# Scores by seven half products, silu read from the banks, and one bank per output tile in a hybrid decoder step

## The chip, the cores and the metric

The kernel runs on one core of one Trainium2 chip. The metric is the device time of one execution in microseconds (us); a time of several runs is their median.

## The reference, cut to what matters

One layer for 2048 new tokens (and 32 sample tokens of running requests), all in float32:

```python
def mixer(xn, s0, lp):
    q, k, v, r, a, u, sv = split_cols(xn @ w_in)
    logg = jax.nn.log_sigmoid(a @ w_alpha + b_alpha) / GLA_TAU
    o, S = gla_chunked(q, k, v, logg, s0)
    o = rmsnorm(o, g_gla_out).reshape(B, T, GLA_WIDTH) * jax.nn.silu(r)
    sv = rmsnorm(jax.nn.gelu(sv).reshape(B, T, SGU_HEADS, SGU_DH), g_sgu)
    s_out = jax.nn.gelu(u) * sgu_spatial(sv, w_s, b_s)
    return jnp.concatenate([o, s_out], axis=-1) @ w_out, S, sv

def mem_attend(hn, mk, mv, wq_x, wo_x):
    s = einsum('bthd,bmhd->bhtm', hn @ wq_x, mk) * MEM_DH ** -0.5
    return einsum('bhtm,bmhd->bthd', softmax(s), mv) @ wo_x

def layer(x, ...):
    h = x + mixer(rmsnorm(x, g_mix), ...)
    h = h + mem_attend(rmsnorm(h, g_x), ...)
    return h + conv_ffn(rmsnorm(h, g_ffn), ...)   # gate, up, causal conv, down
```

The model width is 1024 (eight tiles of 128), the width of the FFN 2816 (22 tiles), and the cross-attention has 4 heads over 256 memory tokens. A last RMS norm gives the output.

## The kernel before, in words

The 2048 tokens go in four blocks, s = 0 to 3, of 512; block 1 carries the 32 sample tokens through the mixer as well (544 columns, in two pieces of 272), block 2 through the FFN. Activations lie with features on partitions and tokens on columns, `B.h[m]` being the residual of feature tile m. Every large product runs on TensorE in three passes, `mm3` (L91 to L94): both operands are split into a high and a low part, and high by high, low by high and high by low are summed in one PSUM bank. `split` (L83) makes the high part on ACT and the low part on DVE. There are two pools of four banks, `acc` for the large sums and `mps` for all else.

A block goes through these stages: the input projections (tiles named t_ws, a_wk, a_wq, t_wv, a_wu, t_wr, and the narrow product `ap` of `a_fn`, L838), into which the steps of GLA (gated linear attention) and of SGU (the spatial gating) are woven; the output projection (a_wo); `stat` (the row sums for the norm); the scores (sc); the turns (transposes of the softmaxed scores, pT); the attention's output (a_wx); the FFN (a_wg, a_wup, then down, d). `weave` (L458) spreads side lists of steps over a main list by their index, and `run` requests the weights of steps ahead of time; behind both, the framework's scheduler lays out each engine's instructions, and each engine then works in that order.

Four places matter below.

*Scores.* In block 0 the memory keys are multiplied into the query weights (`fold_qk`, L595), so that a score is one product of the normed residual with a table `qkd` of 1024 x 512 for each pair of heads. `score(i, j)` adds up, for pair i, eight k-tiles by four token chunks of 128, each mm3 with 512 columns moving: 192 products a block. `soften` reads the banks: row maximum (DVE), exponential (ACT), reciprocal and scaling (DVE).

*Seven products.* The gate and up products of the FFN already go by seven products in place of eight half-size ones, after Strassen: `seven_tokens` (L181) makes, from an even and an odd k-tile of activations, the four sums and their splits that go to the tiles named w, wb, wt and wu.

*r and its silu.* The projection t_wr gives r, token-major, in four `mps` banks. DVE scales them into SBUF (L828, "r<-t_wr"), and later `silu(c)` (L1142) in the tail of GLA applies silu in place on ACT. The tail is: squares of o (ACT, "junk<-o"), `ors` (POOL), the gates (DVE, L1148, o by ors by r), transposes `otp`, and the splits ch and cl that the output projection reads for k-tiles 0 to 3.

*Output projection.* `out_proj_steps` first adds k-tiles 4 to 7 (those of SGU) for all eight output tiles, each half into `h` (L1208): 96 products. Then, in w2, k-tiles 0 to 3, another 96. With `whole=True`, as the attention's output has it, a tile's bank stays open over both halves, and only output tiles 0 to 3 can start early (48 products), since four banks are open.

At the end of the last block, `down_last` does the last two FFN tiles in two token halves, so that `final_steps` (transposes yp, squares, norm, y) of one half can follow while the other is computed.

## Time and profile before

| | |
|---|---|
| median of 3 runs | 2845.88 us (2843.69 to 2846.43) |
| the profiled execution | 2846.04 us |
| its span, first to last instruction | 2844.3 us |
| granted TensorE clock, mean share | 0.997 |
| busy: PE, weight loads (PEld), DVE, ACT, POOL | 99%, 86%, 62%, 37%, 19% |
| main DMA queue, share of 16 engines | 64.6% |

The span lies 1.7 us inside the execution's own time. "Busy" is the time in which at least one instruction of an engine ran; matmuls overlap in their pipeline, so the pace of a run of products is read from the distance between their starts, not from the length of one. A bracket behind a row is the idle time of that engine before it, and the instruction that ended it.

### The profile page before, as it was taken

What the parts mean: (1) busy time and instruction counts of PE and PEld (TensorE: products, weight loads), DVE (VectorE), ACT (ScalarE), POOL (GpSimd) and SP (SyncE); (2) the same over time, 40 slices, a digit from 0 to 9 for tenths busy, and PEclk for the clock granted to TensorE, in tenths of its full rate; (3) what the DMA queues carried; (4) which work ended last, traced back from release to release, by engine and by line L of the source; (5) the groups of instructions that cost most, each with busy time, mean ns of one, the idle gap of its engine ahead of it and who ended that gap; (6) DMA issues with size and microseconds to landing.
All of it is one profiled execution on the core that took longest, in us unless ns stands there. A gap on an engine that the chain in (4) does not pass through costs nothing.

```text
span 2844.3 us, 45766 instructions
## 1 busy us (share of the span) xinstructions
PE 2814.4 (99%) x17366; PEld 2457.6 (86%) x17366; DVE 1773.6 (62%) x3160; ACT 1047.0 (37%) x1942; POOL 542.4 (19%) x617
## 2 busy tenths in 40 slices
...
GB/s 304 207 156 199 208 228 332 335 340 329 345 112 77 94 153 178 302 284 291 329 344 161 73 60 181 191 259 257 257 263 213 104 69 119 185 258 269 273 286 173
DMA packets 363920, 625.54 MB, mean 220 GB/s; under 512 B 26730, under 2 KB 235724, under 8 KB 363702
## 3 DMA queue, kind: packets, MB, share of 16 engines
q1 hardware_dynamic: 363702, 622.62, 64.6%
q8 instruction: 138, 2.26, 0.3%
q14 instruction: 80, 0.66, 0.1%
...
## 4 chain that ended last, share of the span: by engine, by line
PE 95%; DVE 2%; DMA 1%; ACT 1%; issue 1%; POOL 0%; SPq 0%; DVEq 0%; POOLq 0%; ACTq 0%
PE d L92 6%; PE d L94 6%; PE d L93 6%; PE a_wo L92 2%; PE a_wo L94 2%; PE a_wo L93 2%; PE sc L94 2%; PE sc L93 2%; PE sc L92 2%; PE a_wx L93 2%; PE a_wx L94 2%; PE a_wx L92 2%; PE s L1022 2%; PE a_wg L92 1%; PE a_wup L92 1%; PE a_wg L93 1%
## 5 line engine op out<-in xcount | busy, mean ns | idle before, releaser
L92 PE MATMUL d<-acth,whi_wd 128*128 128x512 f32 (+2 forms) x720 | 244.6, 340 | 0.5 <-DVE h L1581 0.5
L93 PE MATMUL d<-actl,whi_wd 128*128 128x512 f32 (+2 forms) x720 | 242.5, 337 | 0.0
L94 PE MATMUL d<-acth,wlo_wd 128*128 128x512 f32 (+2 forms) x720 | 242.0, 337 | 0.0
L1581 DVE TENSOR_TENSOR h<-d,h 128x512 f32<-128x512 f32 (+1 forms) x232 | 133.4, 582 | 139.6 <-PE d L94 139.4
L1520 POOL TENSOR_TENSOR c<-c,bc_f 128x512 f32<-128x512 f32 (+1 forms) x88 | 138.5, 1578 | 137.9 <-ACT c L1519 137.2
L94 PEld LDWEIGHTS d<-acth,wlo_wd 128*128 128x128 f32 x720 | 135.4, 188 | 15.3 <-issue 1.2
L92 PEld LDWEIGHTS d<-acth,whi_wd 128*128 128x128 f32 x720 | 135.3, 188 | 14.4 <-DVE h L1581 0.7
L93 PEld LDWEIGHTS d<-actl,whi_wd 128*128 128x128 f32 x720 | 135.6, 188 | 13.8 <-issue 0.4
L1510 ACT ACTIVATE c<-g,colsb 128x512 f32<-128x512 f32 x88 | 71.7, 815 | 203.7 <-DVE g L1479 151.8
L1542 POOL TENSOR_TENSOR c<-r_q_wup,c 128x512 f32<-128x512 f32 (+1 forms) x33 | 59.1, 1790 | 333.5 <-DVE r_q_wup L279 213.1
L92 PE MATMUL a_wo<-ch,h_wo 128*128 128x512 f32 (+1 forms) x320 | 112.7, 356 | 4.5 <-DVE r L828 4.5
L1507 POOL COPY carry<-g 128x2 f32<-128x2 f32 x88 | 30.7, 349 | 436.5 <-DVE g L1479 434.4
L94 PE MATMUL a_wo<-ch,l_wo 128*128 128x512 f32 (+1 forms) x320 | 112.4, 353 | 0.0
L93 PE MATMUL a_wo<-cl,h_wo 128*128 128x512 f32 (+1 forms) x320 | 112.0, 351 | 0.0
L1511 DVE SCALAR_TENSOR_TENSOR c<-g,colsb,c 128x512 f32<-128x512 f32 x88 | 86.0, 977 | 29.3 <-ACT c L1510 28.8
L92 PE MATMUL sc<-whi_qk,woh 128*128 128x512 f32 x256 | 102.1, 399 | 0.0
L92 PE MATMUL a_wx<-pTh,whi_wx 128*128 128x512 f32 x256 | 101.3, 396 | 0.0
L94 PE MATMUL sc<-whi_qk,wol 128*128 128x512 f32 x256 | 101.1, 397 | 0.0
L93 PE MATMUL a_wx<-pTl,whi_wx 128*128 128x512 f32 x256 | 101.1, 395 | 0.0
L93 PE MATMUL sc<-wlo_qk,woh 128*128 128x512 f32 x256 | 101.0, 395 | 0.0
L94 PE MATMUL a_wx<-pTh,wlo_wx 128*128 128x512 f32 x256 | 100.6, 393 | 0.0
L84 ACT ACTIVATE acth<-c 128x512 fp32r<-128x512 f32 (+1 forms) x88 | 55.9, 636 | 110.4 <-DVE c L1542 85.0
...
## 6 DMA issues: line engine op xcount, KB each, us to landing
...
```

Of the source, the lines that this page charges most:

```text
L84: act.activation(hi, src, AF.Copy)
L92: pe.matmul(ps, wh, xh, start=first, stop=False)
L93: pe.matmul(ps, wh, xl, start=False, stop=False)
L94: pe.matmul(ps, wl, xh, start=False, stop=last)
L1022: pe.matmul(ps3[:, :, c * 64:(c + 1) * 64], kl[:, c * 128:(c + 1) * 128], kr3[:, :, c * 64:(c + 1) * 64], start=True, stop=True)
L1507: pool.tensor_copy(carry[:, f, :], g[:, SB:SB + 2])
L1510: act.activation(c[:, :SB], g[:, 2:SB + 2], AF.Identity, bias=cb, scale=w2)
L1511: dve.scalar_tensor_tensor(c[:, :SB], g[:, 1:SB + 1], w1, c[:, :SB], ALU.mult, ALU.add)
L1520: pool.tensor_tensor(c[:, :T], c[:, :T], B.fbc[:, :T], ALU.mult)
L1542: (dve, pool)[i].tensor_tensor(c[:, :T], q[i], c[:, :T], ALU.mult)
L1581: dve.tensor_tensor(B.h[m + mm][:, cs], ps[:, :cw], B.h[m + mm][:, cs], ALU.add)
```

## The change

Four parts that belong together in the code. The scores use seven products of halves (halves of the tokens, even and odd k-tiles, the two heads of a pair); the table becomes `q7d`, with the plain parts stored split and the sums S1 to S4 stored whole and split when they are loaded; the seven results are put together by additions on DVE into `B.p`, and `soften` reads those. The output projection of blocks 0, 2 and 3 uses `whole`. Silu of r is applied by ACT as it reads the t_wr banks, and the `silu` steps in the tail are gone. The key-value products of GLA for four chunks go into one bank (`states`), the chunks' outputs two to a bank (`chunks`). Besides, `a_fn` stands after the t_ws steps and uses an `mps` bank, and the end of the last block is written differently: the last two FFN tiles token-major (`last_rows`), h transposed ahead (`turn_h`). The core of the diff:

```diff
-    def seven_tokens(a, b, H, name):
+    def seven_tokens(a, b, H, name, apart=False):
...
         lo_, hi_ = slice(0, H), slice(H, 2 * H)
+        one = U(f"w1{name}", F32R)
+        split(one[:, lo_], one[:, hi_], B11)
+        out = {"A11": (one[:, lo_], one[:, hi_])}
         dve.tensor_tensor(t13[:, lo_], B12, B11, ALU.subtract)
+        th, tl = U(f"wth{name}", F32R), U(f"wtl{name}", F32R)
+        if apart:
+            split(th[:, lo_], tl[:, lo_], t13[:, lo_])
         dve.tensor_tensor(t13[:, hi_], B22, B12, ALU.subtract)
         dve.tensor_tensor(t24[:, lo_], B22, t13[:, lo_], ALU.subtract)
         dve.tensor_tensor(t24[:, hi_], B21, t24[:, lo_], ALU.subtract)
-        one = U(f"w1{name}", F32R)
-        split(one[:, lo_], one[:, hi_], B11)
...
-            split(h[:, :2 * H], l[:, :2 * H], src[:, :2 * H])
+        for nm, src, first, second in (("b", b, "A12", "S4"), ("u", t24, "S2", "A22"), ("t", t13, "S1", "S3")):
+            if nm == "t":
+                h, l, c = th, tl, slice(H if apart else 0, 2 * H)
+            else:
+                h, l, c = U(f"w{nm}h{name}", F32R), U(f"w{nm}l{name}", F32R), slice(0, 2 * H)
+            split(h[:, c], l[:, c], src[:, c])
             out[first], out[second] = (h[:, lo_], l[:, lo_]), (h[:, hi_], l[:, hi_])
...
+            t13, t24 = U(f"q13{h}{j}{kk}"), U(f"q24{h}{j}{kk}")
+            dve.tensor_tensor(t13[:, m0], f[:, m0], f[:, m1], ALU.add)
+            dve.tensor_tensor(t13[:, m1], e[:, m0], f[:, m0], ALU.subtract)
+            dve.tensor_tensor(t24[:, m0], t13[:, m0], e[:, m0], ALU.subtract)
+            dve.tensor_tensor(t24[:, m1], e[:, m1], t24[:, m0], ALU.subtract)
+            for i, t in enumerate((t13, t24)):
+                put(sums[:, 2 * i:2 * i + 2, jj], t[:, :512].rearrange("p (s m) -> p s m", s=2))
...
         def a_fn():
             B.aT = T_(f"aT{s}")
             for ci, (c0, cw) in enumerate(chunks_of(sample)):
-                ps = acc(f"ap{s}{ci}")
+                ps = mps(f"ap{s}{ci}")
...
-        out.insert(3, Step(a_fn))
+        out.append(Step(a_fn))
...
-        out += tm_steps(w, R0, xs, sample, ev_tm("r", scaled), f"wr{s}")
+        out += tm_steps(w, R0, xs, sample, ev_tm("r", lambda o, i, f: act.activation(o, i, AF.Silu, scale=f)), f"wr{s}")
...
+        def states(p):
+            kv = mps(f"kv{s}{p}")
+            for c in range(4):
+                for hh in range(2):
+                    h = 2 * p + hh
+                    pe.matmul(kv[hh * 64:(hh + 1) * 64, c * 128:(c + 1) * 128],
+                              B.kt[p][:, c * 128 + hh * 64:c * 128 + (hh + 1) * 64],
+                              B.v[c][:, h * 128:(h + 1) * 128], start=True, stop=True)
+            t = U(f"S{s}{p}")
+            B.S[p] = [state[p]] + [t[:, c * 128:(c + 1) * 128] for c in range(3)]
+            state[p] = cp.tile([128, 128], F32, tag=f"S{p}", name=f"S{s}{p}e", bufs=2)
+            for c in range(4):
+                dve.scalar_tensor_tensor(B.S[p][c + 1] if c < 3 else state[p], B.S[p][c], B.eb[p][:, c:c + 1],
+                                         kv[:, c * 128:(c + 1) * 128], ALU.mult, ALU.add)
...
+        def chunks(p, i):
...
-        def silu(c):
-            n = 128 if c < 4 else NS
-            act.activation(B.r[c][:n, :512], B.r[c][:n, :512], AF.Silu)
...
-            out += [lambda p=p, c=c: chunk(p, c) for c in range(4)]
+            out += [lambda p=p: states(p)] + [lambda p=p, i=i: chunks(p, i) for i in range(2)]
...
-        tail = [onorm] + [lambda c=c: silu(c) for c in range(nt)] + [lambda c=c: gate(c) for c in range(nt)]
+        tail = [onorm] + [lambda c=c: gate(c) for c in range(nt)]
...
-        def score(i, j):
+        SEQ = ("A11", "S1", "A12", "S2", "S3", "S4", "A22")
+        def score(i, nm):
+            plain, sums = q7d[i]
             def fn(wu):
                 wh, wl = wu
...
+                if nm == "A11":
+                    B.p[i], B.ps = [None] * 4, {}
+                ps = B.ps[nm] = acc(f"sc{s}{i}{nm}")
+                for c in range(2):
                     cs = slice(c * 128, (c + 1) * 128)
...
-            return Step(fn, [wready(qkd[i][j], f"qk{s}{i}{j}")])
...
-        def soften(i, c, ps):
...
+                    for k in range(4):
+                        xh, xl = B.hn[k][nm]
+                        mm3(ps[:, c * 256:(c + 1) * 256], xh[:, cs], xl[:, cs], wh[:, k], wl[:, k], k == 0, k == 3)
+                q = B.p[i]
+                plus = lambda o, nm, b: dve.tensor_tensor(q[o][:, :512], B.ps[nm], q[b][:, :512], ALU.add)
+                if nm == "A11":
+                    q[0] = T_(f"p{s}{i}0")
+                    act.activation(q[0][:, :512], ps, AF.Copy)
+                elif nm == "S2":
+                    q[3], q[1] = T_(f"p{s}{i}3"), T_(f"p{s}{i}1")
+                    plus(3, "S2", 0)
+                    plus(0, "A12", 0)
+                    plus(1, "S1", 3)
+                    soften(i, 0)
+                elif nm == "S3":
+                    q[2] = T_(f"p{s}{i}2")
+                    plus(2, "S3", 3)
+                    plus(3, "S3", 1)
+                    soften(i, 3)
+                elif nm == "S4":
+                    plus(1, "S4", 1)
+                    soften(i, 1)
+                elif nm == "A22":
+                    plus(2, "A22", 2)
+                    soften(i, 2)
+            def load():
+                if nm in PLAIN:
+                    return wready(plain[:, PLAIN.index(nm)], f"qk{s}{i}{nm}")()
+                raw = wraw(f"qk{s}{i}{nm}")
+                nc.sync.dma_start(raw[:, :1024], sums[:, SUMS.index(nm)].rearrange("p k m -> p (k m)"))
+                return wsplit(raw[:, :1024].rearrange("p (k m) -> p k m", k=4), f"qk{s}{i}{nm}")
+            return Step(fn, [load])
+        def soften(i, j):
+            mx = narrow(f"mx{s}{i}{j}")
+            p, c0 = B.p[i][j], 2 * (j % 2)
+            dve.tensor_reduce(mx[:, 0:2], p[:, :512].rearrange("p (t m) -> p t m", t=2), AX.X, ALU.max)
+            dve.tensor_tensor(mx[:, 0:2], mx[:, 0:2], B.rn[:, c0:c0 + 2], ALU.mult)
+            for c in range(2):
+                pt = p[:, c * 256:(c + 1) * 256]
+                act.activation(pt, pt, AF.Exp, bias=mx[:, c:c + 1], scale=B.rp[:, c0 + c:c0 + c + 1],
...
+        def turn_h(j):
+            for c in range(4):
+                ps = mps(f"hp{c}{j}")
+                for i in range(4):
+                    pe.transpose(ps[:, i * 128:(i + 1) * 128], B.h[4 * j + i][:, c * 128:(c + 1) * 128], ident)
+                t = U(f"ht{c}{j}")
+                act.activation(t[:, :512], ps, AF.Copy)
+                cur["ht", c, j] = t
+        def last_rows(*ws):
...
+            for c in range(4):
+                cs = slice(c * 128, (c + 1) * 128)
+                ss = narrow(f"yss{s}{c}")
+                for j in range(2):
+                    wh, wl = ws[j]
+                    ps = acc(f"dr{s}{c}{j}")
                     for k in range(2):
...
+                        hi, lo = acts[FT - 2 + k]
+                        mm3(ps, hi[:, cs], lo[:, cs], wh[:, k], wl[:, k], k == 0, k == 1)
+                    y = cur["ht", c, j]
...
+                dve.tensor_tensor(ss[:, 2:3], ss[:, 0:1], ss[:, 1:2], ALU.add)
+                rstd_of(ss[:, 3:4], ss[:, 2:3], 128, 1, 1.0 / D)
+                if ready:
+                    finish(*ready)
+                ready = c, ss
+            finish(*ready)
...
-            if fin and nf == 2:
-                pend = [down_last(f0, lambda half: fin[2 * half:2 * half + 2])]
+            if last and nf == 2:
+                pend = [Step(lambda j=j: turn_h(j)) for j in range(2)]
+                pend.append(Step(last_rows, [wready(wdd[f0, 4 * j], f"wd{s}{f0}{j}") for j in range(2)]))
             else:
...
-                                      lambda B=B: B.cat, "gx", "wo", B.mix_sample, 4, B.mix_sample, keep)
+                                      lambda B=B: B.cat, "gx", "wo", B.mix_sample, 4, B.mix_sample, keep, seven=True, whole=not B.mix_sample)
         folds = [(qk_steps, 0, 10), (vo_steps, 11, 19)] if s == 0 else []
...
-        steps += weave(sc + x1, (turns[:2], 4, 5), (turns[2:], 8, 8))
-        fin = final_steps(B)
...
         else:
-            steps += fmain[-4:] + conv_out_steps(carry, 2, o_state_conv[0, 0], "nc") + flast
+            steps += fmain[-4:-2] + flast[:1] + fmain[-2:] + ncs[4:] + flast[1:]
```

On ACT, in block 2, this is where the tail of GLA begins; `h_wo` is the high part of a weight tile of the output projection, `junk` a square of o, `ch26` and `ch27` are high parts of SGU's outputs. Before:

```order
L84 ACTIVATE ch26_16507<-z22_16504 128x512
L84 ACTIVATE ch27_16549<-z23_16546 128x512
L1142 ACT_TABLE_LOAD
L1142 ACTIVATE r20_16565<-r20_16565 128x512
L1142 ACTIVATE r21_16566<-r21_16566 128x512
L1142 ACTIVATE r22_16567<-r22_16567 128x512
L1142 ACTIVATE r23_16568<-r23_16568 128x512
L84 ACTIVATE h_wo201_16618<-r_wo201_16616 128x1024
L84 ACTIVATE h_wo202_16668<-r_wo202_16666 128x1024
```

And now:

```order
L84 ACTIVATE h_wo242_17148<-r_wo242_17146 128x1024
L879 ACTIVATE junk_90,oss2_17184<-o22_16650 128x128 x2
L84 ACTIVATE ch27_17142<-z23_17139 128x512
L879 ACTIVATE junk_90,oss2_17184<-o22_16650 128x128
L874 ACT_TABLE_LOAD
L874 ACTIVATE r20_17158<-t_wr20_16985,xrs2_15606 128x512
L874 ACTIVATE r21_17159<-t_wr21_16992,xrs2_15606 128x512
L874 ACTIVATE r22_17160<-t_wr22_16999,xrs2_15606 128x512
L874 ACTIVATE r23_17161<-t_wr23_17006,xrs2_15606 128x512
L879 ACTIVATE junk_90,oss2_17184<-o23_16651 128x128 x4
L84 ACTIVATE h_wo202_17215<-r_wo202_17213 128x1024
```

The four activations of r now read the banks `t_wr`, behind one more `h_wo` and the table load, and in front of four squares of o; before they worked in SBUF, and DVE had emptied the banks.

On TensorE, in block 2, the change of the score products, from the last products of the output projection on. Before:

```order
L94 MATMUL a_wo2070_16966<-ch23_16732,l_wo203_16739 128x512
L92 MATMUL sc200_17004<-whi_qk200_16770,woh20_16820 128x512
L93 MATMUL sc200_17004<-wlo_qk200_16772,woh20_16820 128x512
L94 MATMUL sc200_17004<-whi_qk200_16770,wol20_16821 128x512
L92 MATMUL sc200_17004<-whi_qk200_16770,woh21_16842 128x512
L93 MATMUL sc200_17004<-wlo_qk200_16772,woh21_16842 128x512
L94 MATMUL sc200_17004<-whi_qk200_16770,wol21_16843 128x512
L92 MATMUL sc201_17011<-whi_qk200_16770,woh20_16820 128x512
```

And now:

```order
L94 MATMUL a_wo2470_17558<-ch23_17317,l_wo203_17324 128x512
L92 MATMUL sc20A11_17655<-whi_qk20A11_17385,w1wo21_17363 128x256
L93 MATMUL sc20A11_17655<-wlo_qk20A11_17387,w1wo21_17363 128x256
L94 MATMUL sc20A11_17655<-whi_qk20A11_17385,w1wo21_17363 128x256
L92 MATMUL sc20A11_17655<-whi_qk20A11_17385,w1wo23_17424 128x256
L93 MATMUL sc20A11_17655<-wlo_qk20A11_17387,w1wo23_17424 128x256
L94 MATMUL sc20A11_17655<-whi_qk20A11_17385,w1wo23_17424 128x256
L92 MATMUL sc20A11_17655<-whi_qk20A11_17385,w1wo25_17517 128x256
L93 MATMUL sc20A11_17655<-wlo_qk20A11_17387,w1wo25_17517 128x256
L94 MATMUL sc20A11_17655<-whi_qk20A11_17385,w1wo25_17517 128x256
L92 MATMUL sc20S1_17686<-h_qk20S1_17448,wthwo21_17367 128x256
L93 MATMUL sc20S1_17686<-l_qk20S1_17449,wthwo21_17367 128x256
```

Each product now moves 256 columns, not 512; A11 needs the even k-tiles alone, and S1 reads a table part that was split after its load.

## Rows read from the trace of the kernel before

**Rows 1.** The page: busy time by engine, and the chain that ended last.
```profile
PE 2814.4 (99%) x17366; PEld 2457.6 (86%) x17366; DVE 1773.6 (62%) x3160; ACT 1047.0 (37%) x1942; POOL 542.4 (19%) x617
...
PE 95%; DVE 2%; DMA 1%; ACT 1%; issue 1%; POOL 0%; SPq 0%; DVEq 0%; POOLq 0%; ACTq 0%
```

**Rows 2.** TensorE groups by line and shape: busy, mean ns | idle before.
```profile
L92 PE MATMUL sc<-whi_qk,woh 128*128 128x512 f32 x256 | 102.1, 399 | 0.0
...
L92 PE MATMUL a_wo<-ch,h_wo 128*128 128x512 f32 x192 | 75.2, 397 | 4.5 <-DVE r L828 4.5
```

**Rows 3.** Timeline, scores of block 2: start us, length us, engine, line.
```profile
1732.24 0.40 PE L92 MATMUL sc<-whi_qk,woh 128*128 128x512 f32 x1
...
1748.53 0.40 PE L93 MATMUL sc<-wlo_qk,woh 128*128 128x512 f32 x1
```

**Rows 4.** Timeline, gate and up products of block 1, a load (PEld).
```profile
1134.42 0.28 PE L92 MATMUL a_wg10A<-wuh,wg10A 128*128 128x256 f32 x1
...
1134.90 0.19 PEld L94 LDWEIGHTS a_wg10A<-wuh,wg10A 128*128 128x128 f32 x1
...
1138.45 0.28 PE L93 MATMUL a_wup10S<-wtl,h_wup10S 128*128 128x256 f32 x1
```

**Rows 5.** Timeline, TensorE in block 0 before the product `ap`.
```profile
110.76 2.14 PE L840 MATMUL ap<-h,wa 128*32 128x512 f32 x12 [2.26 <-ACT sv L843]
```

**Rows 6.** Timeline, block 2, start of the output projection.
```profile
1669.05 1.06 ACT L84 ACTIVATE h_wo<-r_wo 128x1024 fp32r<-128x1024 f32 x1 [3.79 <-PE t_wr L94]
...
1673.75 0.31 ACT L855 ACTIVATE junk<-o 128x128 bf16<-128x128 f32 x1
...
1674.18 0.31 ACT L855 ACTIVATE junk<-o 128x128 bf16<-128x128 f32 x1
...
1677.32 1.28 ACT L1142 ACT_TABLE_LOAD   x1
1678.62 2.20 ACT L1142 ACTIVATE r<-r 128x512 f32<-128x512 f32 x4
...
1676.14 0.50 PE L92 MATMUL a_wo<-ch,h_wo 128*128 128x512 f32 x1 [1.98 <-DVE r L828]
...
1676.59 2.91 POOL L299 TENSOR_TENSOR ors<-rt,neghalf 128x16 f32<-128x16 f32 x1
```

**Rows 7.** Timeline, the same place in blocks 0 and 1.
```profile
275.73 1.06 ACT L84 ACTIVATE h_wo<-r_wo 128x1024 fp32r<-128x1024 f32 x1
...
276.00 0.50 PE L92 MATMUL a_wo<-ch,h_wo 128*128 128x512 f32 x1 [0.52 <-DVE r L828]
...
976.10 0.60 PE L92 MATMUL a_wo<-ch,h_wo 128*128 128x272 f32 x1
...
976.15 0.66 ACT L84 ACTIVATE ch<-z 128x544 fp32r<-128x544 f32 x1 [2.53 <-POOL z L905]
...
978.86 5.33 DVE L1148 SCALAR_TENSOR_TENSOR o<-o,ors,r 128x128 f32<-128x128 f32 x20 [0.87 <-ACT r L1142]
```

**Rows 8.** Groups of VectorE by line and shape.
```profile
L85 DVE TENSOR_TENSOR l_wo<-r_wo,h_wo 128x1024 fp32r<-128x1024 f32 x32 | 39.2, 1225 | 3.6 <-ACT h_wo L84 3.6
...
L1208 DVE TENSOR_TENSOR h<-a_wo,h 128x512 f32<-128x512 f32 x48 | 32.6, 687 | 28.9 <-PE a_wo L94 28.8
...
L189 DVE TENSOR_TENSOR t<-wxg,t 128x256 f32<-128x256 f32 x8 | 8.9, 1108 | 0.0
...
L85 DVE TENSOR_TENSOR wbl<-wxg,wbh 128x512 fp32r<-128x512 f32 x8 | 5.4, 681 | 0.0
...
L187 DVE TENSOR_TENSOR t<-wxg,wxg 128x256 f32<-128x256 f32 x8 | 3.3, 418 | 1.8 <-ACT wxg L1218 1.8
```

**Rows 9.** Timeline, TensorE at the first gate products of block 2.
```profile
1822.42 0.39 PE L93 MATMUL a_wg20S<-wtl,wg20S 128*128 128x272 f32 x1 [1.01 <-DVE wtl L85]
```

**Rows 10.** Timeline, the last products and the last output rows.
```profile
2833.54 0.28 PE L94 MATMUL d<-acth,wlo_wd 128*128 128x256 f32 x1
...
2839.56 1.41 DVE L1628 SCALAR_TENSOR_TENSOR y<-yp,yss,gf 128x512 f32<-128x512 f32 x2 [0.66 <-POOL yss L299]
```

More of the change, by code (lines that the diff above doesn't have):

```diff
@@ L189, in seven_tokens @@
         dve.tensor_tensor(t24[:, hi_], B21, t24[:, lo_], ALU.subtract)
-        one = U(f"w1{name}", F32R)
-        split(one[:, lo_], one[:, hi_], B11)
-        out = {"A11": (one[:, lo_], one[:, hi_])}
-        for nm, src, first, second in (("b", b, "A12", "S4"), ("t", t13, "S1", "S3"), ("u", t24, "S2", "A22")):
-            h, l = U(f"w{nm}h{name}", F32R), U(f"w{nm}l{name}", F32R)
-            split(h[:, :2 * H], l[:, :2 * H], src[:, :2 * H])
+        for nm, src, first, second in (("b", b, "A12", "S4"), ("u", t24, "S2", "A22"), ("t", t13, "S1", "S3")):
[4 more added lines that the diff above has]
+            split(h[:, c], l[:, c], src[:, c])
             out[first], out[second] = (h[:, lo_], l[:, lo_]), (h[:, hi_], l[:, hi_])
@@ L491, in run @@
             st.fn(*ready.pop(i, []))
-    qkd = [[dp.tile([128, 2, 2, 512], F32, tag=f"qkd{i}{j}", name=f"qkd{i}{j}") for j in range(4)] for i in range(2)]
+    q7d = [(dp.tile([128, 3, 2, 4, 256], F32, tag=f"q7p{i}", name=f"q7p{i}"),
+            dp.tile([128, 4, 4, 256], F32, tag=f"q7s{i}", name=f"q7s{i}")) for i in range(2)]
     kvd = {(nm, h): dp.tile([128, 2, 512], F32, tag=f"{nm}d{h}", name=f"{nm}d{h}") for nm in "kv" for h in range(4)}
@@ L583, in turn_wq @@
         out = []
-        if j == 0:
-            again("k", h)
+        again("k", h)
         for dt in range(2):
@@ L598, in fold_qk @@
         w = mem_st.t.pop(("w", h, j))
+        plain, sums = q7d[h // 2]
         flush()
         for kk in range(2):
+            jj = 2 * j + kk
             ps = mps(f"qkp{h}{j}{kk}")
@@ new lines, in chunks @@
+        def chunks(p, i):
+            if p == 0 and i == 0:
+                B.o = [U(f"o{s}{c}") for c in range(nt)]
+            ps = mps(f"op{s}{p}{i}")
+            for j in range(2):
+                c = 2 * i + j
+                cs = slice(c * 128, (c + 1) * 128)
+                for hh in range(2):
+                    h = 2 * p + hh
+                    os_ = slice(j * 256 + hh * 128, j * 256 + (hh + 1) * 128)
+                    pe.matmul(ps[:, os_], B.P[h][:, cs], B.v[c][:, h * 128:(h + 1) * 128], start=True, stop=False)
+                    pe.matmul(ps[:, os_], B.qz[h][:, cs], B.S[p][c], start=False, stop=True)
+                dve.tensor_copy(B.o[c][:, p * 256:(p + 1) * 256], ps[:, j * 256:(j + 1) * 256])
```

141 lines of the change are left out of this document (63 added, 78 removed).

## The prediction

> **What bounds the kernel now.** I read the page's busy times and its chain first, then the groups of TensorE, then the timeline at each place that the diff touches. TensorE is busy 2814.4 of 2844.3 us and holds 95% of the chain that ended last [rows 1]; VectorE is busy 62%, ACT 37%. So a change is worth what it does to TensorE's work, less what it adds to the few places where TensorE waits. The groups show how few these are [rows 2]: the scores never waited (0.0), the products of the output projection waited 4.5 us in the whole run, for DVE to empty the banks of r. What else runs on DVE, ACT or POOL costs nothing as long as it stays behind TensorE; the change puts much on them, so each addition is held against the TensorE time that covers it.
>
> **Scores.** Now 4 blocks of 192 products with 512 columns, 768 in all (the three groups like the first of [rows 2], 256 each); afterwards 4 blocks of 2 pairs by 7 products by 24, 1344 in all with 256 columns. The price of one is the distance between starts. In block 2's scores 71 products start between 1732.24 and 1748.53 [rows 3]: 16.29/70 = 0.2327 us. Of 256 columns I take the FFN, which already goes by sevens: 35 products from 1134.42 to 1138.45 [rows 4], 4.03/34 = 0.1185 us. So 768 x 0.2327 = 178.7 us become 1344 x 0.1185 = 159.3 us: **-19.4 us**, 4.9 a block. It presupposes that TensorE finds operands and banks in time.
>
> That a product of 256 columns pays for as many weight loads as one of 512 changes nothing in this price: a load takes 0.19 us [rows 4], but the next product starts 0.1185 us after the last, so loads lie beside products and each other. [...]
>
> **Silu of r.** Before, DVE empties the four t_wr banks, TensorE's first a_wo takes one of them, and ACT loads its table and applies silu later, hidden. Now TensorE's first a_wo waits until ACT has done r's first silu, and ACT stands in the order behind other work. In block 2, from the end of TensorE's last t_wr product: h_wo 1.06, two squares (one each 0.435, from the starts at 1673.75 and 1674.18), ch27 about 0.6, a square 0.435, the table load 1.28, one silu 2.20/4 = 0.55 [rows 6]: 4.8 us, during which TensorE has 0.8 us of work left (four small products). The wait is some 4.2 us with the signals, where it was 1.98 [rows 6]: +2.2, and the same in block 3. In block 0 the chain is h_wo from 275.73 (1.06), table, silu: 278.6, where a_wo stood at 276.00 [rows 7]: +2.6. In block 1 ch ends at 976.81, table and silu end at 978.6, a_wo stood at 976.10 [rows 7]: +2.5, and z comes about 0.5 later: +3.0. Together **+10.0**. Bounds: -4.5 (r's waits vanish as those of [rows 2]) to +14 (one more unit of ACT work of 1 us ahead of each); the order decides it, so I stay near its own sum.
>
> **Output projection in one bank.** In blocks 0, 2 and 3 the cover behind which the tail of GLA runs shrinks from 96 products to 48: 48 x 0.2327 = 11.2 us. The tail from the first silu on: three more silus 1.65, four squares 1.74, ors 2.91 [rows 6], 13 of 16 gates before the first transposed tile is whole, 5.33/20 = 0.267 each [rows 7], then transposes, ch, cl and signals, some 2.5: 12.3 us. So a wait of 1.1 us in blocks 2 and 3; in block 0 products of the folded output weights lie between and cover it. **+2.2**; bounds 0 and 6 (gates half as long again, as DVE's additions come out beside POOL's, below). That half of the additions into h fall away (24 x 0.687, [rows 8]) is off the path.
>
> **DVE around the scores.** `seven_tokens` replaces the simple split. Per pair of tiles, four additions and one low part with 256 columns, three low parts of 512. The table sums S1 to S4 are split on load: eight per block, ACT 1.06 and DVE 1.225 [rows 6, 8]. The score stage itself gets 14 additions of 512 a block, 9.6 us at 0.687, in 40 us. That fits; what is tight is the way into it. During w2 TensorE has 144 products, 33.5 us; DVE has 8 additions into h (5.5), four splits of sums (4.9), and four pairs, each 3 x 0.681 + 5 small operations: at 0.418 each 4.1 us, at 1.108 each 7.6 [rows 8]. That makes 26.9 to 40.7 us. The nearest row for how it ends is the same hand-over of this kernel, from the attention's output to the gate products in block 2: TensorE waited 1.01 us for a split of t [rows 9]. There the order of splits was worse (all of b, t, u before use; now A11's and S1's go first), and fewer things stood on DVE. I take 0.5 us a block, **+2.0**, with bounds 0 and 3 us a block.
>
> **The rest.** `ap` waited 2.26 us in block 0 behind the gelus that held its bank [rows 5]; with its own bank and after the t_ws steps it does not: **-2.3**. Key-value products in one run: the same products, one bank; the waits it may remove are under 1 us; 0, bounds -1 and +1. `fold_qk` in block 0 adds 32 additions on DVE (at 0.418 13 us, [rows 8]) and 16 copies on ACT (at 0.55 9 us, [rows 6]), spread over the whole of the block's projections: 0, bound +3. The end: before, 10.8 us pass from the last product of size at 2833.54 to the end of the span, and the last y is begun at 2839.56 [rows 10]. After it come 16 transposes that now lie before the last product (+2.6); behind the last product remain an addition, a square, the norm and one y, and DVE has four y's to catch up on: some 8 us. I take 0, bounds -2 and +2.
>
> **Sum.** -19.4 + 10.0 + 2.2 + 2.0 - 2.3 = -7.5, from the profiled execution's 2846.0: **2838.5 us**. That execution is 0.16 above the median of the runs, which moves nothing.
>
> **Rivals.** (a) *The silus cost little*: squares and h_wo are found done when t_wr ends, so that only the table and one silu remain, 1.8 us: the 10.0 becomes about 3, the tail wait with it 0, and the time 2828 to 2833. For it speaks that ACT is busy only 37%; against it that h_wo waits for the last t_wr product itself (3.79 us in [rows 6]). 0.22. (b) *DVE falls behind before the scores*, and the kernel ends slower. Place: w2. Point: the 33.5 us are full when the small operations take 0.755 us on the mean ((33.5 - 5.5 - 4.9 - 8.2)/20), which is just between the two rows, 0.418 and 1.108. Each 0.1 us more costs 2 us a block, 8 in all; at 0.92 it adds 13 and the time is 2852, at 1.108 2865. For it: both rows are of the same additions, in one kernel. Against it: the longer one is one addition in four. [...] 0.13. (c) *No net change*: the waits at the silus and behind the gates come out at their upper bounds (+14 and +6), and with them -19.4 - 2.3 + 14 + 6 + 2 = 0.3: 2841 to 2849. It is the same mechanism as mine, half as large again. 0.16. [...] [rows 4] speak against it; 0.01. My own case, 2833 to 2843, has 0.48.
>
> **Numbers.** The range 2829 to 2850 takes in (a) but for its lower end, mine and (c), and leaves out (b) and (d). The bound of no change is 0.2%, 5.7 us, about what a measurement here can tell: 2840.2 to 2851.6 about the median of before. Faster: (a) and three quarters of mine, 0.57; the same: a quarter of mine, (c), a little of (b): 0.31; slower: 0.12.
>
> **What would show it.** In the profile after: products of the scores 0.1185 us apart and about 40 us a block; no wait before `ap`; before the first a_wo a wait for ACT's silu of about 4 us in blocks 2 and 3, and 3 in 0 and 1; a wait of about 1 us for ch in the output projection of 2 and 3; at the scores' first products waits under 1 us. I am wrong if TensorE's first scores wait several us for DVE (b), if silu's waits stay near 2 us (a) or exceed 6 (c), or if products of 256 columns start further apart here than in the FFN (d).

## The result and the profile after

The changed kernel is slower: 2852.27 us in the median of 9 runs against 2843.93 of the kernel before beside it, a ratio of 1.0025 [1.0014, 1.0035], some +7 us where -7.5 was forecast. The profiled execution of after took 2847.67 us, span 2845.8; it is the fastest of the nine, so that the stage lengths below show less than the medians do. TensorE's granted clock averaged 0.9939 over the nine runs; the kernel before has 0.9978 over the 17 runs beside e0_again. That is 0.0039 x 2850 = 11 us of clock, an upper estimate, since TensorE may have been idle in a part of it.

The page of after, busy time by engine and the chain, to be held against [rows 1]:

```profile
PE 2799.9 (98%) x17894; PEld 2476.5 (87%) x17894; DVE 1873.0 (66%) x3322; ACT 1120.1 (39%) x2069; POOL 561.6 (20%) x626
...
PE 89%; DVE 5%; ACT 3%; issue 1%; DMA 1%; POOL 1%; SPq 0%; POOLq 0%; ACTq 0%; DVEq 0%
```

TensorE has 14.5 us less work and the span is not shorter; its share of the chain fell from 95% to 89%, and DVE and ACT have the difference. Where, the list of TensorE's waits in after says (releaser: us in total, times, longest):

```profile
PE a_wo L92 <- ACT r L874: 15.9, 4, 4.4
...
PE t_wv L92 <- DVE q L871: 2.0, 1, 2.0
...
PE sc10A L94 <- DVE w1wo L85: 1.0, 1, 1.0
...
PE sc10S L94 <- DVE wtlwo L85: 0.6, 1, 0.6
PE sc10S L92 <- DVE h L1237: 0.6, 1, 0.6
...
PE sc10S L92 <- ACT wthwo L84: 0.6, 1, 0.6
...
PE a_wo L92 <- ACT ch L88: 0.4, 1, 0.4
```

The waits for r are 15.9 us where they were 4.5 [rows 2]; the `ap` wait [rows 5] is gone, a wait for q at t_wv has come; and the scores wait (3.6 us in block 1, under 0.8 in each of the others), which they did nowhere before. The place of [rows 6] in after, block 2, TensorE and ACT by the timeline:

```profile
1676.89 1.04 ACT L84 ACTIVATE h_wo<-r_wo 128x1024 fp32r<-128x1024 f32 x1
...
1677.25 0.39 PE L1128 MATMUL op<-S,qz 128*128 128x128 f32 x2
...
1678.56 0.61 ACT L84 ACTIVATE ch<-z 128x512 fp32r<-128x512 f32 x1
...
1679.49 1.28 ACT L874 ACT_TABLE_LOAD   x1
1680.78 2.42 ACT L874 ACTIVATE r<-t_wr,xrs 128x512 f32<-128x512 f32 x4
...
1681.52 0.80 PE L92 MATMUL a_wo<-ch,h_wo 128*128 128x512 f32 x1 [3.88 <-ACT r L874]
1682.11 0.63 PE L93 MATMUL a_wo<-cl,h_wo 128*128 128x512 f32 x1
```

The queue is the forecast one (h_wo, squares, ch, table, one silu) and the wait, 3.88 us, is near the forecast's 4.2; in blocks 0 and 1 it is 4.4 and 3.7 where about 3 was expected. What the forecast did not have is the length of the products behind it: 0.63 us in place of 0.39. The same stretch by windows of 1 us (busy us of PE, PEld, DVE, ACT, POOL, then the granted clock, DMA share, GB/s):

```profile
1678.00:1679.00 1.00, 0.00 (x0) 0.00 (x0) 1.00 (x2) 0.97 (x5) 0.19 (x1) 1.00 0.00 0
...
1680.00:1681.00 1.00, 0.00 (x0) 0.00 (x0) 0.00 (x0) 0.99 (x2) 0.52 (x1) 0.72 0.74 201
1681.00:1682.00 1.00, 0.48 (x1) 0.48 (x2) 0.00 (x0) 1.00 (x3) 0.00 (x0) 0.50 0.84 291
...
1686.00:1687.00 1.00, 1.00 (x4) 0.81 (x3) 0.00 (x0) 0.00 (x0) 1.00 (x1) 0.50 0.00 0
1687.00:1688.00 1.00, 1.00 (x6) 0.78 (x5) 0.00 (x0) 0.00 (x0) 0.98 (x1) 0.86 0.00 0
```

The clock falls to 0.50 while TensorE sits idle, and comes back at about 1687.3 (0.82 from 1687.20 to 1687.40, then 1.00). The 13 products from 1681.52 on took 5.71 us until 1687.23; at the pitch of [rows 3] they take 13 x 0.2327 = 3.03, so 2.7 us are lost on top of the wait. The first products behind the 3.88 us of idling ran at 0.50. The length of one wait alone does not tell when this happens: after the 1.98 us of [rows 6] the clock stayed at 1.00 in the trace of before, and after the same wait in e13 (told below), behind the same products in the same order, it fell to 0.50. Timeline, then a window, of e13:

```profile
1674.48 0.50 PE L92 MATMUL a_wo<-ch,h_wo 128*128 128x512 f32 x1 [1.98 <-DVE r L828]
```

```profile
1676.00:1679.00 3.00, 3.00 (x8) 2.32 (x8) 1.52 (x2) 2.99 (x5) 3.00 (x2) 0.50 0.00 0
```

The scores' pace in after, block 3, ten products in a row:

```profile
2399.68 0.28 PE L92 MATMUL sc30A<-whi_qk30A,w1wo 128*128 128x256 f32 x1
...
2400.75 0.28 PE L92 MATMUL sc30A<-whi_qk30A,w1wo 128*128 128x256 f32 x1
```

1.07 us for 9 steps are 0.119 us, the forecast's price; rival (d), loads that set the pace, with its chance of 0.01, is out. Yet the stages do not show the forecast's 17.4 us (19.4 less 2.0). From the first products of each class, us, the four blocks added up (projections with the wait before a_wo; the kernels e1, e14 and e11 are told below):

| stretch | before | after | e1_again | e14 | e11 |
|---|---|---|---|---|---|
| t_ws to a_wo | 696.7 | 702.0 | 694.9 | 706.1 | 691.7 |
| a_wo to sc | 193.6 | 202.2 | 199.4 | 202.1 | 196.3 |
| sc to a_wx | 189.5 | 180.2 | 181.6 | 175.1 | 175.1 |
| all else | 1764.6 | 1761.4 | 1764.8 | 1761.1 | 1757.0 |
| span | 2844.3 | 2845.8 | 2840.8 | 2844.5 | 2820.1 |

The spans do not rank the kernels: the execution of after that was profiled is the fastest of its nine, those of e1_again and e14 are the slowest of their eleven.

The scores' stretch of the four blocks went from 47.3, 47.9, 47.3, 47.0 to 43.4, 49.3, 43.3, 44.3: block 1 gained nothing. What stands in its way there, timeline of TensorE, DVE and POOL in block 1 of after:

```profile
1030.14 1.36 POOL L1264 TENSOR_TENSOR wosq<-wosq,woq 128x544 f32<-128x544 f32 x1 [3.52 <-ACT woq L1259]
...
1030.55 1.50 DVE L85 TENSOR_TENSOR wtlwo<-t13wo,wthwo 128x512 fp32r<-128x512 f32 x1
...
1033.75 1.47 POOL L1264 TENSOR_TENSOR wosq<-wosq,woq 128x544 f32<-128x544 f32 x1 [2.24 <-ACT woq L1259]
...
1033.94 1.56 DVE L85 TENSOR_TENSOR w1wo<-wog,w1wo 128x256 fp32r<-128x256 f32 x1
...
1035.56 0.38 PE L94 MATMUL sc10A<-whi_qk10A,w1wo 128*128 128x256 f32 x1 [0.98 <-DVE w1wo L85]
```

Each of DVE's two long operations (low parts of the splits for the scores) was begun while POOL's running sum of squares was under way, and ended 0.55 and 0.28 us after it. With POOL idle, earlier in the same block, they take 0.68 and 0.41 us:

```profile
1026.82 0.68 DVE L85 TENSOR_TENSOR wtlwo<-t13wo,wthwo 128x512 fp32r<-128x512 f32 x1
1027.42 0.41 DVE L85 TENSOR_TENSOR w1wo<-wog,w1wo 128x256 fp32r<-128x256 f32 x1
```

Later in the block it is POOL's sum that gets long: begun at 1042.34, 0.25 us after one of DVE's, it takes 4.21 us, and the operations of DVE there keep their 0.68 and 0.41. The expectations below call this turns.

```profile
1042.09 0.68 DVE L85 TENSOR_TENSOR wtlwo<-t13wo,wthwo 128x512 fp32r<-128x512 f32 x1
...
1042.34 4.21 POOL L1264 TENSOR_TENSOR wosq<-wosq,woq 128x544 f32<-128x544 f32 x1 [2.94 <-ACT woq L1259]
...
1042.70 0.41 DVE L85 TENSOR_TENSOR w1wo<-wog,w1wo 128x256 fp32r<-128x256 f32 x1
```

### The profile page after: what moved, and what is told of

The parts are those of the page before. It is cut to its first block, busy times and chain, and to the rows that moved or that the text cites. A ratio compares the mean times of both kernels' runs of the same rounds, so it can differ in the third digit from the quotient of the medians.

```text
span 2845.8 us, 47247 instructions
## 1 busy us (share of the span) xinstructions
PE 2799.9 (98%) x17894; PEld 2476.5 (87%) x17894; DVE 1873.0 (66%) x3322; ACT 1120.1 (39%) x2069; POOL 561.6 (20%) x626
## 4 chain that ended last, share of the span: by engine, by line
PE 89%; DVE 5%; ACT 3%; issue 1%; DMA 1%; POOL 1%; SPq 0%; POOLq 0%; ACTq 0%; DVEq 0%
PE d L94 6%; PE d L92 6%; PE d L93 6%; PE a_wx L94 2%; PE a_wx L93 2%; PE a_wx L92 2%; PE s L1046 2%; PE a_wg L92 1%; PE a_wup L94 1%; PE a_wg L94 1%; PE a_wup L92 1%; PE a_wg L93 1%; PE a_wup L93 1%; PE a_wo L92 1%; PE a_wo L93 1%
## 5 line engine op out<-in xcount | busy, mean ns | idle before, releaser
L92 PE MATMUL d<-acth,whi_wd 128*128 128x272 f32 (+1 forms) x688 | 235.4, 342 | 0.0
L94 PE MATMUL d<-acth,wlo_wd 128*128 128x272 f32 (+1 forms) x688 | 233.5, 340 | 0.0
L93 PE MATMUL d<-actl,whi_wd 128*128 128x272 f32 (+1 forms) x688 | 233.5, 339 | 0.0
L94 PEld LDWEIGHTS d<-acth,wlo_wd 128*128 128x128 f32 x688 | 129.3, 188 | 15.6 <-issue 1.2
L93 PEld LDWEIGHTS d<-actl,whi_wd 128*128 128x128 f32 x688 | 129.3, 188 | 13.8 <-issue 0.4
L92 PEld LDWEIGHTS d<-acth,whi_wd 128*128 128x128 f32 x688 | 129.3, 188 | 13.5
L92 PE MATMUL a_wo<-ch,h_wo 128*128 128x512 f32 (+1 forms) x320 | 114.6, 367 | 16.3 <-ACT r L874 15.9
L1571 DVE SCALAR_TENSOR_TENSOR c<-g,colsb,c 128x512 f32<-128x512 f32 x88 | 86.0, 978 | 29.1 <-ACT c L1570 28.4
L1579 ACT ACTIVATE c<-c 128x512 f32<-128x512 f32 (+1 forms) x88 | 56.2, 638 | 100.3 <-DVE c L1572 88.3
L1572 DVE SCALAR_TENSOR_TENSOR c<-g,colsb,c 128x512 f32<-128x512 f32 x88 | 91.5, 1040 | 1.1
L92 PEld LDWEIGHTS a_wo<-ch,h_wo 128*128 128x128 f32 x320 | 62.2, 195 | 26.8 <-ACT r L874 17.6
```

The source lines that it names most:

```text
L92: pe.matmul(ps, wh, xh, start=first, stop=False)
L93: pe.matmul(ps, wh, xl, start=False, stop=False)
L94: pe.matmul(ps, wl, xh, start=False, stop=last)
L1571: dve.scalar_tensor_tensor(c[:, :SB], g[:, 1:SB + 1], w1, c[:, :SB], ALU.mult, ALU.add)
L1572: dve.scalar_tensor_tensor(c[:, :SB], g[:, 0:SB], w0, c[:, :SB], ALU.mult, ALU.add)
L1579: act.activation(c[:, :T], c[:, :T], AF.Gelu_apprx_tanh)
```

## The experiments

Two theories stood at first. A: r's silu on ACT, with the clock, makes after slower, and the rest is a gain near the forecast. B: DVE is late for the scores, and the silu matters little. Ratios are to the kernel before, run beside each.

**e0_again.** The kernel after once more.

> The changed kernel unchanged, on the chip of the runs beside it, for a second profile. Theory 1 (the waits for r's silu, and the half clock after them, carry the loss): before the first a_wo of each block a wait for ACT of 3.7 to 4.4 us again, then a granted clock of 0.5 for 3 to 7 us; ratio to before 1.002 to 1.004. Theory 2 (VectorE in the scores and the projections carries it): the same ratio, with the waits in the scores of block 1.

2856.20 us, 1.0037 [1.0024, 1.0051]; span 2855.7, clock 0.993. Same waits for r (4.40 in block 0, 3.88 and 3.87 in 2 and 3). Block 1's scores took 52.4 us here and not 49.3, with the same order of products: behind the waits the clock fell in the scores too. The window of e0_again, TensorE at work all through:

```profile
1050.00:1055.00 5.00, 5.00 (x24) 5.00 (x25) 2.89 (x6) 2.17 (x3) 0.00 (x0) 0.50 0.01 3
```

**e1_dve_r.** r as before, the rest of the change left.

```diff
-ev_tm("r", lambda o, i, f: act.activation(o, i, AF.Silu, scale=f))
+ev_tm("r", scaled)
-tail = [onorm] + [lambda c=c: gate(c) for c in range(nt)]
+tail = [onorm] + [lambda c=c: silu(c) for c in range(nt)] + [lambda c=c: gate(c) for c in range(nt)]
```

> The changed kernel with r scaled out of the banks by VectorE and silu in the tail on ScalarE, as before; all else changed. Theory 1: the four waits before a_wo (15.9 us in all) fall to about 4.5 us as before, the stretches at half clock behind them go, and with 11 us of waits and 5 to 8 us of clock the kernel ends 16 to 20 us under the changed one, 2833 to 2837, ratio to before 0.996 to 0.998. Theory 2: only the waits move, VectorE has four more operations per block in the same place, and the time stays at 2845 to 2850.

2837.45 us, 0.9974 [0.9962, 0.9986]. Waits for r under 0.5 in blocks 0 and 1, 2.35 in 2 and 3. After against this: 0.0051, 14.5 us by the first measurement of after; 0.0063, 18 us, by e0_again, which ran beside it. That is what the silus cost. B falls as the chief cause, but the rest gains 7 us, not 17.5.

**e2_before_act_r.** The kernel before with the silus alone (the reverse of the edit above).

> The kernel before with one edit: r's silu by ScalarE from the banks. Theory 1: the waits before a_wo grow from 4.5 to about 16 us, each is followed by some us at half clock, so 16 to 20 us slower, ratio 1.005 to 1.007. Rival: ScalarE has more room in the kernel before, the waits grow by less than 4 us in all, and the ratio is 1.000 to 1.002.

2859.44 us, 1.0052 [1.0040, 1.0065]: +15 us, the same size from the other side. TensorE's row in block 2:

```profile
1686.80 0.79 PE L92 MATMUL a_wo<-ch,h_wo 128*128 128x512 f32 x1 [5.18 <-ACT r L850]
```

**e3_filler.** After, with 15 products whose result nobody reads ahead of the first a_wo of blocks 1 to 3.

```diff
+if name == "wo" and m2 == 0 and k0 == 4 and s > 0 and begin:
+    fp = mps(f"fill{s}")
+    for i in range(15):
+        pe.matmul(fp, B.xs[6][0][:, :128], B.xs[7][0][:, :512], start=True, stop=True)
```

> The changed kernel with 15 products of 512 columns on operands that lie ready, into a bank that nobody reads, ahead of the first a_wo of blocks 1, 2 and 3: TensorE waits for the same silu, but works for 3.5 us of that time. The clock by itself: if the half clock comes from the idle time, the stretches at 0.5 after the a_wo of blocks 1 to 3 go, a_wo starts within 0.5 us of where it does without, and 5 to 8 us come back against the changed kernel (ratio 0.997 to 0.998 of it). If the clock falls for another reason, the stretches stay and nothing comes back.

2844.95 us, 1.0005 [0.9996, 1.0014]: more work for TensorE, and 6 us less time than the first measurement of after (0.0020), 9 us less than e0_again beside it (0.0032). The timeline of e3 at the place:

```profile
1679.15 3.02 PE L1227 MATMUL fill<-xh,xh 128*128 128x512 f32 x12
1682.59 0.50 PE L92 MATMUL a_wo<-ch,h_wo 128*128 128x512 f32 x1 [0.42 <-ACT r L874]
1682.93 0.39 PE L93 MATMUL a_wo<-cl,h_wo 128*128 128x512 f32 x1
```

Its last t_wr product starts at 1677.42 and a_wo 5.17 us after; in after 1676.35 and 1681.52, also 5.17. So a_wo starts no sooner, but its products run at a granted clock of 1.00 (0.66 in after). The 10 us behind by windows, e3 and then after:

```profile
1680.00:1690.00 10.00, 9.58 (x42) 7.52 (x41) 1.77 (x7) 6.81 (x17) 4.20 (x2) 1.00 0.17 53
```

```profile
1680.00:1690.00 10.00, 8.48 (x25) 6.79 (x26) 2.16 (x9) 4.93 (x14) 3.42 (x2) 0.66 0.17 53
```

Since only the idle stretch was filled, this shows the clock's part in blocks 1 to 3: 6 us of the 14.5, or 9 of the 18.

**e9_act_copy.** After, with ACT scaling r out of the banks without a table, silu later.

```diff
-ev_tm("r", lambda o, i, f: act.activation(o, i, AF.Silu, scale=f))
+ev_tm("r", lambda o, i, f: act.activation(o, i, AF.Copy, scale=f))
```

> As the changed kernel, but ScalarE only scales r out of the banks (no table needed), and silu follows in the tail, in SBUF. It stands in ScalarE's order where r's silu stood, behind h_wo, three squares and ch27, with the table load behind it. If the queue ahead of r makes the wait, 2.6 us are left of 3.9 in blocks 2 and 3 (less the table's 1.28), and the time lies between e1 and the changed kernel, 2840 to 2846. If the table load makes it, the waits fall to about 1 us and the time is that of e1 or lower.

2847.14 us, 1.0009 [1.0000, 1.0017]. Timeline, block 2:

```profile
1682.93 2.40 ACT L874 ACTIVATE r<-t_wr,xrs 128x512 f32<-128x512 f32 x4
...
1683.65 0.50 PE L92 MATMUL a_wo<-ch,h_wo 128*128 128x512 f32 x1 [2.47 <-ACT r L874]
...
1685.63 1.28 ACT L1175 ACT_TABLE_LOAD   x1
```

The wait lost 1.4 of 3.88 us, about the table load's 1.28; 2.5 are the queue ahead of r on ACT.

**e4_whole_off.** e1 with the output projection in two halves again.

```diff
-keep, seven=True, whole=not B.mix_sample)
+keep, seven=True)
```

> As e1 (r by VectorE, all else changed), and the output projection of every block in two separate halves again, as before. My term for the one bank was +2.2 us (waits of 1.1 us for ch in blocks 2 and 3), so this should be 1 to 3 us under e1, with no wait for ch between the halves; if the term was wrong and the shorter cover costs nothing, the same as e1 within 1 us, or above it for the 24 additions into h that come back.

2855.76 us, 1.0042 [1.0030, 1.0055]: 18 us above e1, where 1 to 3 us under it were expected. a_wo to sc is 4 us shorter, as the forecast's shorter cover would have it, but the scores take 50.3, 49.2, 50.0 and 52.0 us: all blocks now look like block 1. TensorE's waits in block 2's scores, timeline:

```profile
1727.29 0.39 PE L92 MATMUL sc20A<-whi_qk20A,wbhwo 128*128 128x256 f32 x1 [1.13 <-DVE h L1241]
...
1731.17 0.39 PE L92 MATMUL sc20S<-h_qk20S,wthwo 128*128 128x256 f32 x1 [0.63 <-ACT wthwo L84]
...
1734.69 0.58 PE L94 MATMUL sc20A<-whi_qk20A,w1wo 128*128 128x256 f32 x1 [0.80 <-DVE w1wo L85]
```

Behind these waits the clock fell here as well: from 1735.07 to 1737.42, and in block 1 from 1035.27 to 1037.62, the products start 0.21 us apart in place of 0.119. Why one bank helps is argued, not shown: with it the eight additions that complete h lie 22.7 to 51.0 us behind the first a_wo of block 2 (e1_again), without it 28.4 to 51.5 (e4), so that the work which hangs on the first tiles can begin 6 us earlier. In block 1, which carries the sample's columns, `whole` is off in every kernel here, and the sevens gain nothing there.

**e5_afn_old.** e1 with `ap` at its old place and bank.

```diff
-ps = mps(f"ap{s}{ci}")
+ps = acc(f"ap{s}{ci}")
-out.append(Step(a_fn))
+out.insert(3, Step(a_fn))
```

> As e1, with the product ap where it was before (ahead of the last t_ws step, in a bank of the large pool). Block 0 should lose 2.3 us of wait and some 1.7 us of clock again; block 1 should get back its wait of 1.95 us for VectorE's q, since VectorE's order there then has q between the scalings of sv again. Theory 1 (the q wait comes from this move): the two cancel, and the time is that of e1 within 2 us, with the wait gone from block 1 and back in block 0. Rival: the q wait stays, and the time is 3 to 4 us above e1.

2838.83 us, 0.9983 [0.9974, 0.9992], not to be told from e1. Block 0's wait is back (2.49 us, clock 0.57 in the 10 us behind it), and block 1's wait of 1.95 for q is gone: the new place pays in block 0 and costs in block 1.

**e6_no_yg.** e1 without the product that POOL takes from DVE at the end (`yg`).

> As e1, without GpSimd's product of h and the final gain in the last rows: VectorE makes that y too. In e1 two y's of VectorE that lie beside the GpSimd product take 2.41 us where two others take 1.42. If GpSimd's operation held VectorE up, the two take 1.42 us, one y of 0.75 comes on top, and the end is 0 to 0.5 us earlier; if the 2.41 us have another cause, they stay and the end is 0.7 us later.

2837.12 us, 0.9970 [0.9959, 0.9981], as e1. The timelines of after, and then of e6:

```profile
2835.45 2.41 DVE L1632 SCALAR_TENSOR_TENSOR y<-ht,yss,gf 128x512 f32<-128x512 f32 x2
2835.61 1.70 POOL L1656 TENSOR_TENSOR yg<-ht,gf 128x512 f32<-128x512 f32 x1 [0.79 <-DVE ht L1652]
...
2835.80 0.40 PE L94 MATMUL dr<-whi_wd,actl 128*128 128x512 f32 x1
```

```profile
2827.31 1.41 DVE L1633 SCALAR_TENSOR_TENSOR y<-ht,yss,gf 128x512 f32<-128x512 f32 x2
```

POOL's product costs DVE 1.0 us (2.41 against 1.41), about what it saves, one y of 0.7.

**e7_e1_filler** (e1 with 8 such unread products in blocks 2 and 3) and **e8_best** (e7 with `ap` at its new place in block 0 only).

> As e1, with 8 products on ready operands into an unread bank ahead of the first a_wo of blocks 2 and 3, where TensorE waits 2.35 us for VectorE's r. If idle time is what lowers the clock, the half clock behind these waits (e1 shows 0.83 in one 10 us window of block 2, 0.90 and 0.92 in two of block 3, some 3.5 us lost) goes, and the kernel is 2 to 4 us under e1; if not, the same as e1 or slower by what the products push back a_wo.

> As e7 (r by VectorE, 8 products in the waits of blocks 2 and 3), with the new place and bank of ap in block 0 alone and the old ones in blocks 1 to 3. Block 1's wait of 1.93 us for VectorE's q and the half clock behind it (0.83 in one 10 us window) should go, and block 0's wait before ap not come back: 3 to 4 us under e7, 2832 to 2834. If the q wait has nothing to do with ap's place in block 1, the same as e7.

2836.84 us, 0.9972 [0.9961, 0.9982], and 2835.41 us, 0.9965 [0.9954, 0.9977]. In e8 t_wv of block 1 starts without a wait. The steps are too small to tell from e1 singly; e8 beats both kernels.

**e10_kv_old** and **e1_again.** e1 with the key-value products chunk by chunk as before, and e1 beside it.

```diff
-out += [lambda p=p: states(p)] + [lambda p=p, i=i: chunks(p, i) for i in range(2)]
+out += [lambda p=p, c=c: chunk(p, c) for c in range(4)]
```

> The kernel of e1_dve_r with the key-value products chunk by chunk as before. In the kernel after, the projections of blocks 2 and 3 came 2.3 and 3.3 us sooner than before, for which the forecast had nothing (key-value products in one run: 0, with bounds of -1 and +1). If the one run is what shortened them, TensorE's stretch from the first product of t_ws to the first of a_wo is 2 to 3 us longer in each of blocks 2 and 3 than in e1_dve_r, and the time 4 to 6 us above it (ratio to before about 0.999). If the run is worth what the forecast said, the time stays within 1.5 us of e1_dve_r (ratio 0.997 to 0.998) and the stretches within 0.5 us.

> The kernel of e1_dve_r once more, beside e10_kv_old on the same chip: ratio 0.9974 as before, within 0.0015.

e10 2843.95 us, 0.9996 [0.9987, 1.0005]; e1 again 2838.91, 0.9975 [0.9966, 0.9984]. Without the wait for r, t_ws to a_wo takes 150.8 and 152.8 us in blocks 2 and 3 of e10, 148.6 and 150.7 in e1_again. Timeline of e10, a group of four, and of e1_again, a run of sixteen:

```profile
1666.70 0.39 PE L94 MATMUL t_wr<-h_wr,xl 128*128 128x512 f32 x1
1667.01 0.44 PE L1113 MATMUL kv<-v,kt 128*64 128x128 f32 x4
1667.38 0.49 PE L1107 MATMUL op<-v,P 128*128 128x128 f32 x2
```

```profile
1664.95 0.39 PE L93 MATMUL t_wr<-l_wr,xh 128*128 128x512 f32 x1
1665.27 1.09 PE L1104 MATMUL kv<-v,kt 128*64 128x128 f32 x16
1666.30 0.49 PE L1127 MATMUL op<-v,P 128*128 128x128 f32 x2
```

Four products take 0.37 us (0.09 each), sixteen 1.03 (0.064 each), and each entry comes 0.31 to 0.32 after the last t_wr product in place of 0.23. Eight groups a block against two are 8 x (0.37 + 0.08) - 2 x (1.03 + 0.09) = 1.4 us of the 2.2; the rest stays open.

**e11_sq_dve, e12_sq_none, e8_again.** What makes DVE late: the running sums of squares of both norms, moved from POOL to DVE (e11), or left out (e12).

```diff
-pool.tensor_tensor(B.sq[:, :T], B.sq[:, :T], t[:, :T], ALU.add)
+dve.tensor_tensor(B.sq[:, :T], B.sq[:, :T], t[:, :T], ALU.add)
```

> The kernel of e8_best with the running sum of squares of both norms added by VectorE in place of POOL (7 operations for each norm of a block). If VectorE is late in block 1's scores because its two-operand operations and POOL's sums take turns (1.50 and 1.56 us there beside sums of 1.36 and 1.47, 0.68 and 0.41 without), each moved operation costs VectorE 0.43 to 0.69 us and saves it up to 1.1: the long ones go, TensorE's waits in block 1's scores fall from about 3.1 us to under 2, ratio 0.9950 to 0.9965. If the number of operations is what makes it late, the waits grow by some us and the ratio is 0.997 or more.

> The kernel of e8_best without the running sums: the statistic of both norms takes the squares of the first tile alone (so the norms' scales are not the reference's). If the shared turns make VectorE late, the waits of TensorE in block 1's scores are under 1 us and the ratio is 0.994 to 0.996; if the number of operations does, the waits stay at about 3 us and the ratio at 0.9965.

> The kernel of e8_best once more, beside the other two on the same chip: ratio 0.9965 as before, within 0.0015.

e11 2823.57 us, 0.9922 [0.9910, 0.9935]; e12 2820.68, 0.9916 [0.9904, 0.9928]; e8 again 2833.52, 0.9957 [0.9944, 0.9971]. Block 1's scores take 46.3 us in e11 (waits of 0.8 and 0.6 left) and 42.6 in e12 (none), 49.1 in e8_again. The gain of e11, 0.0035 or 10 us, is larger than that: against e8_again the scores of the four blocks fell by 4.6 us in the profiles (179.7 to 175.1), 2.8 of it in block 1; the projections fell by 4.0 and all else by 5.9. The scheduler's order on TensorE moves with this edit too; that part was not separated.

**e13_before_sq_dve, e14_after_sq_dve.** The same line alone, in the kernel before and in the kernel after.

> The kernel before with the running sums of squares of both norms on VectorE. Its scores never waited, so if the gain of e11_sq_dve is that of the seven products' additions coming in time, little is to be had here: only the FFN's entry, 0 to 4 us, ratio 0.9985 to 1.000. If the sums on POOL cost every kernel the same, the ratio is about 0.9965.

> The kernel after with that edit alone. If VectorE's turns with POOL took part of the scores' term, the time falls by 8 to 11 us to about 2842 (ratio 0.9985 to 1.000) and the scores of block 1 take some 46 us in place of 49; if e11_sq_dve's gain came from its other edits together with this one, it stays above 1.001.

e13 2843.25 us, 0.9998 [0.9989, 1.0007]; e14 2843.65 us, 0.9994 [0.9985, 1.0002]. Nothing in the kernel before; in the kernel after 9 us against its first measurement (0.0031), 12 against e0_again (0.0043). Block 1's scores fall from 49.3 to 46.1 us, those of all blocks by 5.1; here too TensorE's order moved with the edit, which was not separated. The pages' busy times of e13 and e14:

```profile
PE 2814.1 (99%) x17366; PEld 2458.1 (86%) x17366; DVE 1776.2 (62%) x3216; ACT 1049.8 (37%) x1942; POOL 471.1 (17%) x561
```

```profile
PE 2799.4 (98%) x17894; PEld 2477.4 (87%) x17894; DVE 1851.7 (65%) x3378; ACT 1122.4 (39%) x2069; POOL 484.0 (17%) x570
```

In e14 DVE does 56 operations more than in after (some 39 us by their groups' means of 0.69 to 0.73) and is busy 21 us less, so that its other operations take some 60 us less, an estimate from these two figures. In e13 the same 56 operations raise DVE's busy time by 2.6 us only [rows 1], so POOL's sums made DVE's operations longer before too; no product of the scores waited for them. One group of DVE by line and shape, after and then e14 (busy us, mean ns):

```profile
L85 DVE TENSOR_TENSOR w1wo<-wog,w1wo 128x256 fp32r<-128x256 f32 x16 | 13.9, 870 | 5.2 <-ACT w1wo L84 5.0
```

```profile
L85 DVE TENSOR_TENSOR w1wo<-wog,w1wo 128x256 fp32r<-128x256 f32 x16 | 7.0, 437 | 0.1
```

The mean falls from 870 ns to 437 with these sums off POOL.

## Why the prediction was wrong

Term by term, forecast against the difference that the runs gave (ratios times 2845 us):

- **Scores, DVE's way into them, one bank, the end**: -19.4 + 2.0 + 2.2 + 0 = -15.2 forecast. e1 gained 7.4 us in all, of which the key-value run is 6.0 (e10) and `ap` 2.6 (e5): what is left for these four terms is -7.4 + 6.0 + 2.6 = +1, give or take some 6 us. In the profile of e1_again the misses lie in the scores (181.6 against 170.1 + 2.0: 9.5 us), from a_wo to sc (199.4 against 193.6 + 2.2: 3.6) and at the end (360.3 against 357.4: 2.9). This is the step that failed, and in it the +2.0 above all, "I take 0.5 us a block". The price of a product was right (0.119), and so were the 14 additions, 0.67 to 0.69 us each in after, with no score product waiting for them. But 189.5 - 19.4 is 170.1 us of scores, and after has 180.2: the stretch lost 10 us where 2 were allowed, 6 of them in block 1. Some 0.6 a block are other products that lie in it (e14's blocks without a wait take 43.0). The rest was lost inside the scores and not at their first products: splits that take 0.68 and 0.41 us with POOL idle took 1.50 and 1.56 beside POOL's sums, products wait for them, and in some executions the clock falls behind the waits (0.50 in e0_again). e14 gives 5 us of the 10 back with one line (175.1). Rival (b), DVE late because its small operations come out long, was the nearest to this; I put it in the wrong place, w2, and gave it 0.13. (Its 1.108 us is the mean of eight additions in before: six that were begun during one of POOL's sums took 1.00 to 1.52 us, the other two 0.42. Its turning point is (33.5 - 5.5 - 4.9 - 8.2)/20 = 0.745 us, not 0.755; that moves nothing.)
- **One bank**: the forecast saw only the shorter cover (+2.2). A longer way from a_wo to sc is there (4 us, e4), but the chief effect has the other sign: without the one bank the kernel loses 18 us, in the scores.
- **Silu of r**: +10.0 forecast for the waits, and 15.9 - 4.5 = 11.4 us is what they grew by. The term measured 14.5 to 18 (e1), 15 (e2). The missing piece is TensorE's clock after each wait (a mean of 0.71, 0.83, 0.66 and 0.83 over 10 us at the waits of blocks 0 to 3 in after), which the working never priced; filling the idle time gives back 6 to 9 us (e3). The granted clock bears it out: 0.9939 in after, 0.9959 in e1, 0.0020 x 2850 = 6 us. Of what e1 still lacks against before (0.9978, 5 us) a part lies in block 1's scores.
- **`ap`**: -2.3 forecast; -2.6 measured, which e5's noise does not tell from 0, as the sum of a gain in block 0 and a new wait in block 1 that was not foreseen.
- **Key-value run**: 0 with bounds of -1 and +1; measured -6.0 (-5.0 by the medians). In the profiles it shows in blocks 2 and 3 alone, and not in their waits; fewer changes between kinds of products account for an estimated 1.4 of 2.2 us a block, from e10's and e1_again's rows.
- **The end**: "some 8 us" behind the last product; it took 10.0 (2835.80 to 2845.8). With 2.6 us of transposes ahead of it, the last FFN stage grew from 357.4 to 359.6 us. A part is POOL's yg (1.0); the rest stays open.

The differences add up to the 14.6 us between forecast and result, but by construction, since the four terms were given what e1's gain leaves over: that is no proof of any of them; a difference of two ratios here is good to some 4 us. Rivals (a) and (d) are refuted by the wait of 3.88 us and the pitch of 0.119. Rival (c) came near in the time (2849 at most) for another reason: r's waits grew by 11.4 us and not by 14, and the waits for ch behind the gates were 0.4 us in all, not 6. The gates half as long again, on which that 6 rested, do not show in after: its gates take 0.33 to 0.35 us each in every block.
